# Cutting the last slab's first load at 14 of 16 rows, and storing the first slab of a pair in one DMA

## The chip, the cores and the metric

One core of one Trainium2 chip. The metric is the device time of one execution in microseconds (us); lower is better. All runs told of here were in the fast state, and all results were correct.

## The reference

The input is 96 images (32 x 3) of 256 x 256 float32; each is turned by 90 degrees.

```python
def setup_inputs():
    batch, c, h, w = 32, 3, 256, 256
    return {"x": np.random.randn(batch, c, h, w).astype(np.float32)}

def reference(x):
    return np.rot90(x, k=-1, axes=(-2, -1)).astype(np.float32)
```

There is no arithmetic. 25.17 MB are read, rearranged on the chip and 25.17 MB are written.

## The kernel before

The images are cut into 12 slabs of 2 MiB. All slabs fit on the chip at once, so the DMA queue first takes all loads, then all stores; VectorE transposes a slab while others are in flight, and ScalarE makes one last pair of copies. A slab is moved in one of two forms: "short" is 8 rows a partition on 128 partitions, 8 KB a packet; "long" is 16 rows a partition on 64 partitions, as two DMAs (`i` = 0, 1) of 1 MiB with 16 KB a packet. Slabs 0 to 2 are loaded short and stored long, 3 to 7 the other way round, 8 to 11 long both ways.

```python
    long_st = (0, 1, 2)
    both = (8, 10)                       # slabs 8, 9 and 10, 11 are turned in pairs
    paired = [n + a for n in both for a in range(2)]
    # ... (views, tiles, pools)
    for n in (0, 1, 2, 3, 7, 4, 5, 6, *range(8, n_slabs)):
        # ... slabs 1 and 2: one DMA each
        for i in range(I):
            if n in long_st:
                ld = nc.sync.dma_start(out=fours(units[n])[:, i], in_=ld_short[n][:, i])
            else:
                ld = nc.sync.dma_start(out=units[n][i::I], in_=ld_long[n, i])
            if (n, i) == (last, 0):
                mark = ld
    # ... turn(n): the transposes of a slab or a pair
    def store(n):
        if n in paired:
            first = n if n in both else n - 1
            for i in range(I):
                nc.sync.dma_start(out=st_long[n, i], in_=pairs[both.index(first)][n - first :: I, i])
        # ... other slabs
    # ...
    for n in (4, 3, 5, 6, 7, 1, 2):
        st = store(n)
        if n == 4:
            tc.add_manual_dep(st.ins, mark.ins.name, ...)   # "stores after loads"
    for n in range(both[0], n_slabs):
        turn(n)
        store(n)
    # ... slab 0 last, through ScalarE
```

The mark: the first store on the queue (slab 4's) does not wait for its own data, which VectorE has ready at about 46.7 us, but for the first of the last slab's two loads to land.

## Time and profile before

| | before |
|---|---|
| time, median of 3 runs | 123.25 us (123.25 to 123.33) |
| span of the profiled run | 121.5 us |
| bytes moved | 50.33 MB |
| DMA packets | 4752, of which 656 are completions of 4 bytes (41 DMAs x 16 engines) |
| VectorE | busy 90.6 us, done at 99 us |

From the page of the kernel before:

```profile
DVE 90.6 (75%) x24; ACT 4.9 (4%) x3; POOL 0.2 (0%) x4
...
DMA packets 4752, 50.33 MB, mean 414 GB/s; under 512 B 656, under 2 KB 656, under 8 KB 656
```

50.33 MB at 428 GB/s alone are 117.6 us. The rest is start and end: the first packet runs at 1.8 us, the rate is still 139 GB/s from 2 to 3 us, the last one ends at 120.3 us, its completion is seen at 120.65 us and the span closes 0.85 us later. A DMA's issue is an instruction of the queue's sequencer; its bytes move later, on 16 DMA engines (most loads land 19.6 us after their issue). Two readings must be kept apart from here on: "no engine idle" (at every moment 16 packets are on record) and "no packet stretched" (a 16 KB packet takes its usual 611 or 612 ns).

### The profile page before, as it was taken

The page shows a single profiled execution, that of the slowest core. Times are in us where ns is not written, and L with a number is a line of the kernel's source. Part 1 is how long each engine was busy: PE and PEld are TensorE (multiplying, and loading weights), DVE is VectorE, ACT ScalarE, POOL GpSimd, SP SyncE. Part 2 cuts the span into 40 slices and gives each one's busy share as a digit, 9 for nine tenths or more (in the row PEclk, how much of TensorE's full clock was granted, in tenths as well). Part 3 has the DMA queues.
Part 4 walks back from the last instruction along what each step waited for, and adds up shares of the span by engine and source line. Part 5 has one row for each costly group of instructions (what it writes and reads, how often), then busy time and mean ns, then how long its engine had stood idle before and what let it go on. Part 6 is the DMA issues. An engine that isn't in the chain of part 4 may idle for free.

```text
span 121.5 us, 134 instructions
## 1 busy us (share of the span) xinstructions
DVE 90.6 (75%) x24; ACT 4.9 (4%) x3; POOL 0.2 (0%) x4
## 2 busy tenths in 40 slices
DVE  0029999999999999999999999999999960000000
ACT  0000000000000000000040000000000038000000
POOL 0000000000000000000000000000000000000000
DMA  3999999999999999999999999999999999999994
GB/s 73 426 429 426 432 458 426 426 421 421 432 432 432 421 432 432 426 426 432 432 405 426 421 429 431 432 423 431 453 432 432 432 432 432 432 432 432 432 432 173
DMA packets 4752, 50.33 MB, mean 414 GB/s; under 512 B 656, under 2 KB 656, under 8 KB 656
## 3 DMA queue, kind: packets, MB, share of 16 engines
q1 hardware_dynamic: 4752, 50.33, 97.9%
HBM read 25.17 MB, written 25.17 MB: 414 GB/s over the span
## 4 chain that ended last, share of the span: by engine, by line
DVE 59%; issue 13%; DMA 6%; DVEq 3%; ACT 2%; ACTq 1%; SPq 0%
DVE u L116 53%; DVE turned L116 6%; DMA u<-in_x_dram 6%; DVEq L169 3%; ACT u L141 2%; ACTq L169 1%; SPq L92 0%; DVEq L116 0%
## 5 line engine op out<-in xcount | busy, mean ns | idle before, releaser
L116 DVE STREAM_TRANSPOSE u<-u 128x2048 f32<-128x2048 f32 x22 | 83.5, 3866 | 0.3
L116 DVE STREAM_TRANSPOSE turned<-u 128x2048 f32<-128x2048 f32 x2 | 7.1, 3586 | 8.2 <-DMA u<-in_x_dram 8.2
L141 ACT COPY u<-turned 128x2048 f32<-128x2048 f32 x2 | 3.6, 1869 | 35.6 <-DVE u L116 35.6
L141 ACT ACT_TABLE_LOAD x1 | 1.3, 1283 | 62.2 <-DMA u<-in_x_dram 62.2
L158 POOL MEMSET const-bfloat16-1.0<- 128x1 bf16 x1 | 0.1, 101 | 0.0
L158 POOL MEMSET const-uint8-127<- 128x1 uint8 x1 | 0.1, 101 | 0.0
L158 POOL MEMSET const-float32-0.0<- 128x1 f32 x1 | 0.1, 98 | 0.2 <-issue 0.2
L158 POOL MEMSET const-float32-1.0<- 128x1 f32 x1 | 0.1, 98 | 0.0
## 6 DMA issues: line engine op xcount, KB each, us to landing
u<-in_x_dram SPq DMA_DIRECT2D x20, 1024.0 KB, 19.6
out_dram<-u SPq DMA_DIRECT2D x14, 1024.0 KB, 15.6
out_dram<-u SPq DMA_DIRECT2D x5, 2048.0 KB, 16.0
u<-in_x_dram SPq DMA_DIRECT2D x2, 2048.0 KB, 13.7
```

Of the source, the lines that this page charges most:

```text
L116: nc.vector.transpose(out=dst[:, h * step : (h + 1) * step], in_=src[:, h * step : (h + 1) * step])
L141: nc.scalar.copy(out=fours(units[last])[:, i], in_=fours(turned0)[:, i])
L158: nc = _bacc.Bacc("TRN2", target_bir_lowering=False, num_devices=1)
L169: with _tile.TileContext(nc) as tc:
```

## The change

Its intent: let the first store start a little earlier, so that the engines never run dry between loads and stores, without giving up the order "stores after loads"; and issue fewer, larger stores for the pairs.

```diff
             if n in long_st:
                 ld = nc.sync.dma_start(out=fours(units[n])[:, i], in_=ld_short[n][:, i])
             else:
-                ld = nc.sync.dma_start(out=units[n][i::I], in_=ld_long[n, i])
-            if (n, i) == (last, 0):
-                mark = ld
+                cuts = (0, 14 * W, RL * W) if (n, i) == (last, 0) else (0, RL * W)
+                for f0, f1 in zip(cuts, cuts[1:]):
+                    ld = nc.sync.dma_start(out=units[n][i::I, f0:f1], in_=ld_long[n, i][:, f0:f1])
+                    if f1 == 14 * W:
+                        mark = ld
 ...
         if n in paired:
             first = n if n in both else n - 1
+            if n == first:
+                nc.sync.dma_start(out=st_long[n].transpose([1, 0, 2]), in_=pairs[both.index(n)][::I])
+                return
             for i in range(I):
```

## The prediction

> **What bounds the kernel now.** I read the page from the top: the span is 121.5 us, the timed median 123.25 us, so 1.75 us lie outside the span and nothing in the change touches them. Then the 40 slices, the queue and the issues.
>
> ```profile
> DVE  0029999999999999999999999999999960000000
> DMA  3999999999999999999999999999999999999994
> GB/s 73 426 429 426 432 458 426 426 421 421 432 432 432 421 432 432 426 426 432 432 405 426 421 429 431 432 423 431 453 432 432 432 432 432 432 432 432 432 432 173
> ...
> q1 hardware_dynamic: 4752, 50.33, 97.9%
> ...
> u<-in_x_dram SPq DMA_DIRECT2D x20, 1024.0 KB, 19.6
> out_dram<-u SPq DMA_DIRECT2D x14, 1024.0 KB, 15.6
> out_dram<-u SPq DMA_DIRECT2D x5, 2048.0 KB, 16.0
> u<-in_x_dram SPq DMA_DIRECT2D x2, 2048.0 KB, 13.7
> ```
>
> The reader is to see one full row, DMA, from slice 1 to 38, while VectorE stops at about 99 us and the rest of the span, 22 us, is DMA alone. The DMA engines are taken for 97.9% of the whole span. The chain of waits gives 59% of the span to VectorE, and I do not follow it: it walks back through transposes, but when the last transpose ends the queue still holds stores for 20 us. What has to move is 50.33 MB, and only fewer bytes, a higher rate or less idle time of the 16 engines can shorten it.
>
> So the question is whether the engines ever idle at the places that the change touches. The stage table around the change from loads to stores, at about 61 us (columns: stretch, its length, busy time of VectorE, ScalarE and GpSimd, TensorE clock, DMA share, GB/s):
>
> ```profile
> 20.00:60.00 40.00, 39.83 (x11) 0.00 (x0) 0.00 (x0) 1.00 1.01 428
> 60.00:62.00 2.00, 2.00 (x1) 0.00 (x0) 0.00 (x0) 1.00 0.96 406
> 62.00:102.00 40.00, 37.03 (x11) 4.12 (x3) 0.00 (x0) 1.00 1.01 431
> 61.00:61.50 0.50, 0.50 (x1) 0.00 (x0) 0.00 (x0) 1.00 0.71 295
> 57.00:57.50 0.50, 0.50 (x1) 0.00 (x0) 0.00 (x0) 1.00 1.15 492
> ```
>
> At first sight there is a dent where stores take over: 406 against 428 GB/s over 2 us, worst 295 in half a microsecond. That dent is what the change aims at, worth about 2 x (1 - 406/428) = 0.10 us. But the last row warns of the reading: a share of 1.15 of 16 engines is impossible, so a packet is put down whole in the stretch in which it starts, and the sizes change here (16 KB load packets, about 0.61 us each, to 8 KB store packets, about 0.31 us). I therefore followed the trace's packet records engine by engine. Each engine ends its last load's packet, then its 4-byte completion packet (9 ns on record, about 6 ns to the next start), and its first 8 KB store packet starts 6 ns after that completion packet starts; the earliest engine does this at 61.17 us and the latest at 61.69 us. No engine has a gap there. Nor is there one over 0.03 us anywhere from 18 us to 120.2 us. The dent is binning, not idleness.
>
> How near the store was to being late is the other half. The queue's waits and the timeline:
>
> ```profile
> SPq L94 <- DMA u<-in_x_dram: 30.5, 13, 4.5
> SPq L122 <- DVE u L116: 18.0, 2, 9.6
> SPq L127 <- DMA u<-in_x_dram: 16.7, 1, 16.7
> ```
>
> ```profile
> 0.72 0.88 SPq L92 DMA_DIRECT2D u<-in_x_dram  x2
> ...
> 59.77 10.88 SPq L127 DMA_DIRECT2D out_dram<-u  x5
> 62.24 1.28 ACT L141 ACT_TABLE_LOAD   x1 [62.24 <-DMA u<-in_x_dram]
> ```
>
> The first store is held 16.7 us (the deliberate "stores after loads") and issued at 59.77 us, when the first of the last slab's two loads has landed; the second lands at 62.24 us, 2.47 us later, which is one 1 MiB load at this rate. At the start of the kernel the first load is issued at 0.72 us and the trace's first packet starts at 1.77 us: 1.05 us from issue to data. So store packets could flow from 59.77 + 1.05 = 60.82 us, and the earliest engine runs out of loads at 61.17 us. The margin is already +0.35 us.
>
> **What the Trainium skill says.** "DMA: Bandwidth & Descriptors", section "Where 436 GB/s comes from", puts the ceiling of one core's 16 engines at 435 GB/s; the 428 and 431 GB/s above are 98 to 99% of it, so the trace agrees and there is no rate left to gain. The same page, "Anatomy of one DMA", says the DMA engines never wait on semaphores, only the issuing sequencer does, and that a completion comes after the last byte is confirmed landed: in the trace the mark load's completion packets run at 58.71 to 59.24 us and the wait ends at 59.77 us. Its section on why a DMA increments its semaphore by 16 says the engine count is the largest number up to 16 that divides the slowest dimension: 64 partitions give 16, in the split loads and in the merged store (64 x 2 x 4096, partition outermost); the 656 small packets of the page are 41 DMAs x 16, which agrees. "Perfetto Trace Analysis", section "DMA Optimizations", warns of overhead for DMAs under 2 KB; the new small load moves 2 rows x 1 KB = 2 KB a packet, on that border, and no row of this trace shows that size.
>
> **The change, part by part.** The order of instructions on every engine but the DMA queue's is the same: 24 transposes, 2 copies, unchanged shapes. On the queue there are 40 DMAs for 41.
>
> (1) The mark covers 14 of 16 rows. It lands 2/16 of a load earlier: 2.45 us x 1/8 = 0.31 us, so the first store should be issued at about 59.47 us and the margin becomes 0.66 us. Gain on the path: 0, because the engines had no gap to fill.
>
> (2) The split adds 64 packets, 4 an engine. A 16 KB packet takes 0.612 us, two 8 KB ones 2 x 0.306 us from start to start, so a packet's own overhead is below what I can see, some 5 ns. 4 x 5 ns = 0.02 us, plus one completion packet of 6 ns. All of this is on the path, as every engine's time is: +0.03 us.
>
> (3) Two merged stores remove two completions an engine: -2 x 6 ns = -0.012 us. Packets (16 KB) and bytes stay. They remove two issues, of 0.47 to 1.39 us each, but the issuing queue runs ahead: when the second pair's stores are issued at 99.16 us, 18 MiB have been asked for and (99.16 - 61.4)/2.447 = 15.4 MiB have been moved, so 2.6 MiB or 6.3 us lie in the queue; at the first pair's, 84.73 us, 14 - 9.5 = 4.5 MiB or 11 us. Gain on the path: 0. The stores still wait for all four transposes of their pair, so no transfer starts earlier.
>
> (4) The eight completion semaphores are handed round, so each DMA from the split on waits for another earlier one, eight back. All of those landed long before (loads take 19.6 us to land when eight are queued; the small one shortens the queue by under 1 MiB). Cost 0.
>
> Sum: +0.03 - 0.01 = +0.02 us. 123.25 + 0.02 = 123.27; I round to 123.25, as the three runs before spread over 0.08 us.
>
> **The rivals.** (A) The dent is a real bubble, or one exists in the timed executions that the profiled one does not show: then an earlier first store fills up to 0.10 to 0.15 us and the time is 123.1. For it: the 295 GB/s slice, and that somebody chose 14 rows. Against it: the packet records, the +0.35 us margin and the tight 123.25 to 123.33. (B) The 2 KB packets are dear: if each held an engine as long as an 8 KB one, 4 x (0.31 - 0.08) = 0.9 us, 124.2; at 40 ns extra each 0.16 us, 123.4. Against it: size scaling from 16 to 8 KB is exact. (C) The merged store, with two distant output regions interleaved a partition at a time, could write slower: 5% on two stores of 4.9 us is 0.5 us, 123.7. Against it: the 2 MiB stores of the first stage also have two regions and run at the same 431 GB/s. (D) The longer issue of a merged store starves the queue: it would need over 6.3 us, and issues take at most 1.4 us a MiB.
>
> **Range and chances.** Rival A pulls 0.15 us down, B and C at their mild sizes 0.15 to 0.2 us up, and a run can sit 0.1 us off by itself: 123.0 to 123.45. A gain of over 2% would be 2.4 us, but all idle time of the DMA engines in the whole span is 2.1% of 121.5 = 2.6 us, nearly all in the first 3 and last 1.3 us, which the change does not touch: chance 0.01. A loss of 2.4 us needs B and C at full size and more: 0.01. Within 2%: 0.98.
>
> **What would show it.** In the changed kernel's trace the first store should be issued at 59.4 to 59.5 us, its wait shortened to about 16.4 us, and the last load should still land at 62.2 to 62.3 us. The GB/s dent at 61 us should remain, perhaps moved, because it is the change of packet size; if it is gone and the span is 0.1 us shorter, rival A was right. DMA packets should be 4752 + 64 - 16 = 4800, of which 640 under 512 B, with some 64 more under 8 KB; the queue's share stays at 97.9% give or take 0.2. The last copy's stores and the end of the span should stay at 121.5 us. A span longer by over 0.2 us with a higher share in the slice before 61 us speaks for B, with a lower GB/s from 85 to 110 us for C.

## The result, and the profile after

| | before | after |
|---|---|---|
| time, median of 6 runs | 123.25 us (123.20 to 123.62) | 123.21 us (123.14 to 123.44) |
| ratio | 1 | 0.9994, 95% interval 0.998 to 1.0007 |
| span of the profiled run | 121.5 us | 121.4 us |

All outputs are right. A ratio here is the mean time of one kernel's runs over the mean of the other's in the same rounds, so it is not quite the ratio of the medians. The verdict is "same".

The page after, its lines that answer to those of before:

```profile
DMA  3999999999999999999999999999999999999994
GB/s 84 416 432 424 426 459 432 432 432 426 426 432 426 416 421 432 421 426 450 403 424 426 426 429 429 421 432 424 464 426 432 432 432 432 432 432 432 432 432 178
DMA packets 4800, 50.33 MB, mean 414 GB/s; under 512 B 640, under 2 KB 640, under 8 KB 704
...
q1 hardware_dynamic: 4800, 50.33, 98.0%
...
out_dram<-u SPq DMA_DIRECT2D x7, 2048.0 KB, 16.3
...
u<-in_x_dram SPq DMA_DIRECT2D x1, 896.0 KB, 19.3
u<-in_x_dram SPq DMA_DIRECT2D x1, 128.0 KB, 17.2
```

The two pieces are there (896 KB and 128 KB), so are the two merged stores (seven of 2 MiB, five before), and the packets are the 4800 that were counted ahead. The DMA row and the bandwidth are those of before. The stages around the change from loads to stores (stretch, length, VectorE, ScalarE, GpSimd, clock, DMA share, GB/s):

```profile
20.00:60.00 40.00, 39.83 (x11) 0.00 (x0) 0.00 (x0) 1.00 1.00 426
60.00:62.00 2.00, 2.00 (x1) 0.00 (x0) 0.00 (x0) 1.00 0.94 397
62.00:102.00 40.00, 36.97 (x11) 4.18 (x3) 0.00 (x0) 1.00 1.02 432
61.00:61.50 0.50, 0.50 (x1) 0.00 (x0) 0.00 (x0) 1.00 0.40 164
```

The dent at 61 us is deeper than before (164 against 295 GB/s, 397 against 406 over 2 us) in a kernel that is no slower, and the packet records show 16 packets under way throughout. A dent that grows while nothing idles is a matter of which packet starts in which slice: a DMA share of 0.40 over half a microsecond does not show an idle engine. The queue's waits and the timeline after:

```profile
SPq L96 <- DMA u<-in_x_dram: 32.5, 14, 4.5
...
SPq L132 <- DMA u<-in_x_dram: 13.9, 1, 13.9
```

```profile
59.46 11.13 SPq L132 DMA_DIRECT2D out_dram<-u  x5
62.26 1.28 ACT L146 ACT_TABLE_LOAD   x1 [62.26 <-DMA u<-in_x_dram]
```

The first store is issued at 59.46 us, 0.31 us ahead of before, and the last load lands at 62.26 us against 62.24 us: the lead did not bring the last load in sooner, and the extra pieces cost it 0.02 us.

### The profile page after: what moved, and what is told of

Its sections match the earlier page's. It is cut to its first block, busy times and chain, and to the rows that moved or that the text cites. A ratio compares the mean times of both kernels' runs of the same rounds, so it can differ in the third digit from the quotient of the medians.

```text
span 121.4 us, 134 instructions
## 1 busy us (share of the span) xinstructions
DVE 90.5 (75%) x24; ACT 4.9 (4%) x3; POOL 0.2 (0%) x4
## 4 chain that ended last, share of the span: by engine, by line
DVE 55%; issue 17%; DMA 6%; DVEq 3%; ACT 2%; ACTq 1%; SPq 0%
DVE u L118 50%; DVE turned L118 6%; DMA u<-in_x_dram 6%; DVEq L174 3%; ACT u L146 2%; ACTq L174 1%; SPq L92 0%; DVEq L118 0%
```

## The experiments

Twelve kernels were run. Each differs from the kernel before, unless told otherwise, by the edit shown. "Issued at" is the first slab 4 store's issue, which is what most of them move. Statements on packets and landings come from one profiled execution of each kernel.

### Each half of the change alone

The load split alone (the diff above without its store part):

> The load split alone, stores as before. My theory (the 16 DMA engines have no gap where stores take over from loads): within 0.1 us of the kernel before, worked out as +0.03 us; first store issued at 59.46 us, last load landing at 62.26 us as in the changed kernel. Rival A (the dent in GB/s at 61 us was an idle stretch that the split fills): 0.10 to 0.15 us faster than before, and a dent that is gone.

Measured: 123.39 us (123.29 to 123.48) against 123.29 us, ratio 1.0004 (0.9992 to 1.0016). Issued at 59.40 us.

The merged store alone:

> The merged store alone, loads and mark as before (first store issued at 59.77 us). My theory: within 0.1 us of before, worked out as -0.01 us. Observed after the prediction: in the changed kernel the 16 engines end their last store at slightly more different moments (119.8 to 120.3 us) than before (120.15 to 120.3 us), with a mean about 0.17 us earlier. If the merged store does that, this run shows it and the split alone does not; the end, set by the slowest engine, should still move by under 0.1 us. Rival C (two output regions interleaved write slower): 0.2 to 0.5 us slower.

Measured: 123.26 us against 123.29 us, ratio 0.9995 (0.9982 to 1.0008). Issued at 59.81 us. Neither half moves the time, so the result is not a gain and a loss that cancel. What I had supposed of the merged store found no support: the profiled run of the merged store alone does not end with an earlier mean over the engines (120.61 us, against 120.57 us before and 120.40 us after), while the split alone does (120.38 us). In these profiles the small shift goes with the earlier issue; but the profiled run of the merged store alone was the slowest of its six (123.66 us), so the comparison is a weak one. It is taken up below.

Both slabs of each pair merged, on top of the changed kernel:

```diff
-            if n == first:
-                nc.sync.dma_start(out=st_long[n].transpose([1, 0, 2]), in_=pairs[both.index(n)][::I])
-                return
-            for i in range(I):
-                nc.sync.dma_start(out=st_long[n, i], in_=pairs[both.index(first)][n - first :: I, i])
+            nc.sync.dma_start(out=st_long[n].transpose([1, 0, 2]), in_=pairs[both.index(first)][n - first :: I])
+            return
```

> The changed kernel with both slabs of each pair stored in one 2 MiB store, so four merged stores and 38 DMAs. My theory: bytes and packets are the same, four completions fewer an engine than before the split, so within 0.1 us of the kernel before. If interleaving two output regions cost something (rival C): 0.2 us or more slower. If fewer, larger stores helped: at least 0.1 us faster.

Measured: 123.32 us (123.25 to 123.39) against 123.28 us, ratio 0.9994 (0.9975 to 1.0013). Four merged stores are worth as little as two. Rival C, at 0.2 us or more, is out: the upper ends of the two intervals are +0.10 us (two merged stores) and +0.16 us (four).

### A late first store, so that a real gap can be seen

The first try held only slab 4's store until the very last load:

```diff
-            if (n, i) == (last, 0):
+            if (n, i) == (last, 1):
                 mark = ld
```

> The first store waits for the last load instead of the one before it. My theory of the margin (1.05 us from issue to first data; engines run out of loads between 61.17 and 61.69 us): the first store is issued at about 62.25 us, its data start at about 63.3 us, so a real gap of 1.6 us (slowest engine) to 2.1 us (earliest engine) opens, and the time is 124.8 to 125.4 us. If instead the kernel had slack elsewhere in the DMA stage, or the chain of waits through VectorE set the end, the time would stay within 0.3 us of 123.25.

Measured: 123.44 us, ratio 1.0008 (0.9993 to 1.0023). This did not test what it was meant to: with that mark the schedule put another slab's store, which has no mark, first, and issued it at 45.03 us. It queued behind the loads, so the engines had work when the loads ended. The second try holds every early store (this edit comes on top of the one above):

```diff
-        st = store(n)
-        if n == 4:
+        for st in store(n):          # store() returns the list of its DMAs
             tc.add_manual_dep(st.ins, mark.ins.name, ...
```

> Repeats the late mark, this time with every store held (in the earlier try the schedule issued another unit's store at 45.03 us, so nothing was late). All stores wait for the last load. My theory of the margin: first store issued at about 62.2 us, its data at about 63.25 us (1.05 us later, as at the start of the kernel), while the engines run out of loads at 61.2 to 61.7 us: a gap of about 2.1 us for the earliest engine and 1.6 us for the latest, time 124.8 to 125.4 us. If the chain through VectorE or slack elsewhere set the end: within 0.3 us of 123.25.

Measured: 125.67 us (125.58 to 125.69) against 123.34 us, ratio 1.018 (1.0156 to 1.0204). From its timeline and its stages:

```profile
62.03 8.36 SPq L126 DMA_DIRECT2D out_dram<-u  x5
```

```profile
61.00:63.00 2.00, 1.97 (x2) 0.95 (x1) 0.00 (x0) 1.00 0.08 33
67.00:87.00 20.00, 19.93 (x6) 0.00 (x0) 0.00 (x0) 1.00 1.01 419
```

This is what a true gap looks like: DMA share 0.08 and 33 GB/s for two microseconds. The store was issued at 62.03 us and its first packet runs at 62.94 us, so 0.91 us lie between. The engines ran out at 61.14 to 61.50 us; in engine time 1.63 us were idle. The kernel lost 2.3 us, more than the idle time, and the second line shows where most of the rest went: from 67 to 87 us, with all engines busy, it moves 419 GB/s where the kernel before moves 430. The same two stretches of the kernel before:

```profile
61.00:63.00 2.00, 1.97 (x2) 0.76 (x1) 0.00 (x0) 1.00 0.93 393
67.00:87.00 20.00, 19.93 (x6) 0.00 (x0) 0.00 (x0) 1.00 1.02 430
```

The landings agree: 19.93 us from the first store to the fifth, against 19.50 us before. Half that delay, with every early store held as in the last edit:

```diff
+                cuts = (0, 8 * W, RL * W) if (n, i) == (last, 1) else (0, RL * W)   # mark: the first half
```

> The second load of the last slab cut at 8 rows, every store waits for its first half: the first store is issued 1.22 us later than before, at about 61.0 us, its data at about 62.05 us. My theory of the margin: gaps of about 0.9 us on the earliest engine and 0.35 us on the latest, time 123.6 to 124.2 us. If issue-to-data inside the running queue is shorter than 1.05 us, less.

Measured: 124.54 us (124.50 to 124.87), ratio 1.0096 (1.007 to 1.0121); issued at 60.98 us, first packet at 61.89 us, again 0.91 us. Idle engine time is 0.49 us, the loss 1.2 us. My number was too small again, for the same reason: idle time plus slower stores afterwards (19.89 us from the first store to the fifth).

And a delay that should still have been inside the margin, again with every early store held:

```diff
+                cuts = (0, 2 * W, RL * W) if (n, i) == (last, 1) else (0, RL * W)   # mark: the 2 rows
```

> The other edge of the window: the second load of the last slab cut at 2 rows, every store waits for its small first piece, so the first store is issued about 0.33 us later than in the kernel before, at about 60.1 us. The late runs measured 0.91 us from the first store's issue to its first packet, so data from about 61.0 us, while the engines run out of loads between 61.15 and 61.7 us. My theory of the margin: still no idle engine, time within 0.15 us of before. If the margin of the kernel before were only the few hundredths of a microsecond that rival A needs: idle time at 61 us and 0.2 us or more slower.

Measured: 123.64 us (123.62 to 123.73) against 123.26 us, ratio 1.0032 (1.0018 to 1.0046). Issued at 60.08 us. Half of the expectation held: 16 packets are on record at every moment, so there is no gap. The other half did not: all five executions are 0.36 us or more above the median of before. The loss lies in the store stage. In the traces' completion records (mean over the 16 engines) the first five stores take 19.64 us from the first landing to the fifth, against 19.50 us before, and the last 10 MiB 24.54 us against 24.48 us; the first store lands at 66.82 us in both kernels, the last one at 120.85 us against 120.57 us. The edit also cuts the second load and ties every early store to the mark; neither was run without the delay.

### An early first store

```diff
-            if (n, i) == (last, 0):
+            if (n, i) == (last - 1, 1):
                 mark = ld
```

> The first store waits for the load before the mark, one load of 2.45 us earlier than in the kernel before, eight times as much lead as the split gives. My theory: first store issued at about 57.3 us, time unchanged, within 0.1 us of before. Rival A (a bubble that an earlier first store fills): at least 0.10 us faster. A third possibility, that stores issued among loads disturb the loads: slower by 0.2 us or more.

Measured: 123.54 us (123.48 to 123.64), ratio 1.0018 (1.0003 to 1.0032). Eight times the change's lead gains nothing, which speaks against rival A from the other side; the third possibility came true. Load packets of 16 KB, normally 611 ns, take up to 985 ns from 60.1 us on (0.17 us an engine in sum above 612 ns). Then only the first store early, the rest at the old mark:

> As the earlier mark, but only the first store goes a load early (57.3 us); the others wait for the mark of the kernel before (59.77 us). If the 0.18% of the earlier mark came from the number of stores queued behind unfinished loads (three 2 MiB stores), the stretched load packets at 60 us (up to 985 ns, normal 611) should be gone or a few, time within 0.1 us of before. If one early store is enough, they stay and the time is 0.15 to 0.3 us above before.

Measured: 123.71 us (123.65 to 123.79), ratio 1.0026 (1.0002 to 1.0049). One early store is enough; the number of queued stores is not the cause. The loss is a little above what I gave for this case, and the packets are stretched from 59.0 us on, 0.39 us an engine in sum. The split at 2 rows and at 8 rows of the last slab's first load (the change's edit with 2 or 8 for 14, no merged store) lie between:

> The split at 2 rows, mark on the small first piece: the first store is issued 2.1 us ahead of before, at about 57.6 us, with a load and seven eighths still to come. Between 1.22 us of lead (same time) and 2.45 us (0.18% slower): if the lead itself is what disturbs the last loads, stretched load packets near 60 us and 0.1 to 0.25 us above before; if not, within 0.1 us.

Measured: 123.49 us (123.35 to 123.73), ratio 1.0008 (0.9979 to 1.0036): inconclusive in time. The trace has stretched load packets after 60 us, 0.10 us an engine in sum.

> The split at 8 rows instead of 14, mark on the first half, stores as before: the first store is issued about 1.22 us ahead of the kernel before (58.5 us), between the 0.31 us of the change and the 2.45 us of the earlier mark, which was 0.18% slower and whose trace has load packets of up to 985 ns (normal 611) once stores were queued. If stores queued early stretch the loads' last packets, some such packets show after 60 us and the time is 0.05 to 0.25 us above before; if the slowness of the earlier mark was chance, no packet over 640 ns and the time within 0.1 us.

Measured: 123.27 us (123.23 to 123.36), ratio 0.9988 (0.9967 to 1.0009), and no packet is stretched. Seen in the stages, 57 to 62 us, of the kernel before, the earlier mark, the single early store, the 2-row split and the 8-row split, one line each in that order:

```profile
57.00:62.00 5.00, 5.00 (x2) 0.00 (x0) 0.00 (x0) 1.00 0.99 421
```

```profile
57.00:62.00 5.00, 5.00 (x2) 0.00 (x0) 0.00 (x0) 1.00 0.99 406
```

```profile
57.00:62.00 5.00, 5.00 (x2) 0.00 (x0) 0.00 (x0) 1.00 0.97 377
```

```profile
57.00:62.00 5.00, 5.00 (x2) 0.00 (x0) 0.00 (x0) 1.00 0.94 389
```

```profile
57.00:62.00 5.00, 5.00 (x2) 0.00 (x0) 0.00 (x0) 1.00 1.01 424
```

The share stays between 0.94 and 1 while the rate falls from 421 to 406, 377 and 389 GB/s: engines that are mostly busy with slow packets, where the late store showed engines with none. The rates do not rank the losses: a packet counts whole where it starts, so an edge of the stretch alone can shift such a rate by tens of GB/s (16 packets of 16 KB are 0.26 MB, 52 GB/s over 5 us). The packet records are firmer. They also hold short gaps, which the kernels issued from 58.5 to 60.1 us do not have: 0.08 us an engine in sum for the earlier mark, 0.05 for the single early store and 0.11 for the 2-row split.

The mis-scheduled late mark above is an early store too, queued 14.7 us ahead of the kernel before, though of another slab. It stretched the load packets less (0.03 us an engine in sum, none over 775 ns), and its ratio of 1.0008 is not clear of noise. So the length of the lead alone does not set the stretch.

### What a small packet costs

The last slab's first load in eight pieces of 2 rows, mark on the seventh:

```diff
+                cuts = tuple(range(0, RL * W + 1, 2 * W)) if (n, i) == (last, 0) else (0, RL * W)
```

> The last slab's first load in eight pieces of 2 rows (2 KB packets), mark on the seventh. The changed kernel's trace has 2 KB packets at 84 ns against 611 / 8 = 76.4 ns for the same bytes in a 16 KB packet. My theory of packet overhead: 32 packets an engine x 7.6 ns = 0.24 us plus 7 more completions x 6 ns = 0.04 us, so 0.28 us slower than the kernel before (123.5). If small packets cost nothing on the path: within 0.1 us. If issue or the eight completion semaphores bind instead: a gap before the next load and over 0.5 us slower.

Measured: 124.88 us (124.33 to 125.76), ratio 1.0119 (1.0084 to 1.0154). The size of the small packets was right: the eight pieces land one after the other in 2.71 us where the whole load takes 2.45 us, so 0.27 us more, against my 0.28 us. But the third alternative held as well. Each DMA waits for the one eight places back, and the load after the pieces now waits for the first of them, which has landed on all engines at 57.71 us. From the timeline of this run:

```profile
57.39 1.11 SPq L96 DMA_DIRECT2D u<-in_x_dram  x2
59.76 1.79 SPq L129 DMA_DIRECT2D out_dram<-u  x3
```

The last piece and the last load are issued from 57.39 us on, the load itself at 57.91 us; in the kernel before it was queued at 42.57 us. Its first packets take 1.05 to 1.34 us on most engines instead of 0.61 us, and the worst engine ends its last load 2.4 us after the same load of the kernel before. Idle engine time is only 0.33 us, so most of the loss sits inside packets that are on record. (The profiled execution is the slowest of the six, 125.76 us; part of its loss is one engine that ends 1.1 us after the other fifteen.) The long packets look as if a packet's record can include a wait, which is inferred, not shown. A missing gap is to be believed only where the packets also have their usual length, as they have before and after.

### All of them along one axis

| kernel | first store issued, us | time, us | last 10 MiB of stores, us |
|---|---|---|---|
| one store early | 57.26 | 123.71 | 24.35 |
| earlier mark | 57.28 | 123.54 | 24.35 |
| mark at 2 rows | 57.61 | 123.49 | 24.34 |
| mark at 8 rows | 58.49 | 123.27 | 24.34 |
| split alone | 59.40 | 123.39 | 24.33 |
| changed kernel | 59.46 | 123.21 | 24.33 |
| all pair stores merged | 59.46 | 123.32 | 24.31 |
| before | 59.77 | 123.25 | 24.48 |
| merged store alone | 59.81 | 123.26 | 24.49 |
| slightly late | 60.08 | 123.64 | 24.54 |
| half a load late | 60.98 | 124.54 | 24.55 |
| after the last load | 62.03 | 125.67 | 24.57 |

(The last column is from one profiled run each: mean landing of the last store less that of the store ten 1 MiB earlier. Times of different rows are from different chips in part; compare through the ratios above. The mis-scheduled late mark, 24.34 us, and the eight pieces, 24.39 us, are left out: in the one another slab is stored first, in the other the last load comes late.) The time is flat from 58.5 to 59.8 us and rises on both sides. The kernel before sits on the late end of the flat part, the changed one inside it.

## Why the prediction was right

A forecast of "no change" comes true easily; what tests its mechanism are the runs that moved the first store on purpose.

**The engines had no gap to fill (the reading of the dent, and part 1).** Right, and shown from both sides: an earlier issue by 0.3, 1.3 and 2.5 us did not make the kernel faster beyond noise, and where there was a gap (after the last load), share and rate fell to 0.08 and 33 GB/s over two microseconds. The first store came at 59.46 us for a predicted 59.47.

**The margin of 0.35 us.** Right in kind, mis-sized in its term. I took 1.05 us from issue to data from the first load of the kernel; a store needs 0.91 us in both late runs, which makes the margin 0.49 us on the earliest engine. What the prediction did not have is that no idle engine is not yet no loss: the store issued 0.31 us later leaves no gap and still costs 0.3%.

**The cost of the split (part 2).** Predicted +0.03 us. The 2 KB packets are on record with 84 ns against 611 / 8 = 76 ns, so 8 ns each and not 5; from seven extra pieces the cost is 0.27 / 7 = 0.04 us a piece. In the time of the whole kernel that is too small to be seen. (The skill's passage on DMAs under 2 KB speaks of whole DMAs; the prediction read it for packets. No DMA here is that small.)

**The merged stores (part 3).** Predicted -0.01 us; two and four of them show nothing within intervals of 0.13% and 0.19% either side. Issues were indeed off the path: in the three kernels with merged stores no engine idles from 18 to 119.7 us. One slip in the reading: the last 22 us are not DMA alone, since ScalarE copies until 102.8 us; nothing in the sum rests on it.

**The completion semaphores (part 4).** Cost 0, right for one extra DMA. One forecast of detail missed through it: I expected the wait of the first store at 16.4 us, and the view shows 13.9 us. The last load's issue moved one landing later (45.02 us instead of 42.57 us), so the wait began later. Eight pieces show where this stops being free. (The skill's "Anatomy of one DMA", which the prediction leans on, is written for DMAs issued from GpSimd; this kernel issues from SyncE, and its trace shows the same order, completion packets at 58.71 to 59.24 us and the end of the wait at 59.77 us.)

**Rivals.** A (a real bubble), B (dear small packets) and C (slower interleaved stores) each got a run of their own, and none holds at the size that the prediction gave it for this change. A is the closest call: 0.10 us is about what the times can resolve (the interval of the split alone reaches down to -0.10 us, that of the 8-row split to -0.41 us), and what speaks against it are the packet records of one execution, with no idle engine, and the longer leads that gain nothing more. D (a long issue starves the queue) falls with the traces: a merged store's issue takes 0.60 to 1.41 us, against the 6.3 us that D needs.

**What stays open.** Two small losses have no cause shown; their shapes differ.

First, an early store. Why it stretches the last loads' packets is open, but the traces show how the loss reaches the end: it leaves the engines uneven. In the run with the earlier mark the 16 engines' landings lie 0.31 us apart at the last load but one, 0.57 us at the last load, and 0.75 us at the last store. That last store lands at 120.63 us in the mean over the engines, hardly later than before (120.57 us), but at 120.99 us on the slowest, against 120.65 us. The single early store shows the same (120.65 and 121.06 us). The slowest engine sets the time. The change fits this: its last store lands 0.17 us sooner in the mean, but 0.03 us sooner on the slowest engine.

Second, after a late first store all engines run slower: 19.64 to 19.93 us from the first store to the fifth against 19.50 us before, 24.54 to 24.57 us for the last 10 MiB against 24.48 us. That column separates cleanly at 59.5 to 59.8 us. In the slow traces the 16 engines' landings lie close together at the end (within 0.17 to 0.22 us, except 0.50 us in the merged store alone; 0.36 to 0.76 us in the kernels issued before 59.5 us). That the closeness causes the slowness is only argued.

The medians hide one thing more. Over all rounds, kernels with the old mark (before, and merged store alone) gave 10 of 54 executions at 123.6 us or more, up to 123.93, while the four kernels issued between 58.4 and 59.5 us gave none in 24, with 123.48 as the highest. That count was made after the fact and over several chips; it suggests that the change removes occasional slow executions, and it is not a result of the paired rounds. The closeness does not explain it as far as can be seen: the only one of the ten that has a trace (merged store alone, 123.66 us) ends at 120.61 us in the mean, as before, with one engine 0.30 us behind the other fifteen.

No version that was tried beats both kernels beyond noise. With 117.6 us of bytes at the engines' rate and a start and end that no edit here touches, there is little left for one to gain.

## What to carry to other kernels

Before tuning a hand-over between loads and stores, look at the packets there, not at a rate by slices: a dent in GB/s can be a change of packet size. Over half a microsecond even the DMA share misleads (0.40 here with no engine idle); over two microseconds a true gap was plain (0.08). Where the engines had no gap, an earlier issue gained nothing in time. It bought margin, and only up to a point: in two runs too early cost 0.2 to 0.3%, and too late cost 0.3% before any engine idled. Look at the slowest engine and not at the mean, too, since it sets the end. Cutting a load was cheap here, at 0.04 us a piece, as long as the number of DMAs allowed in flight did not push a later load's issue onto the path.

## What the Trainium skill lacked or had wrong

- "DMA: Bandwidth & Descriptors", section "Latency and other measured facts", gives about 600 ns to the first byte for DMAs of this kind, and does not say from where it counts. Here 0.91 us lie between the start of a store's issue and its first packet (two runs), and 1.05 us for the first load; from the end of the issuing instruction, which takes about 0.4 us, they are 0.5 and 0.6 us. So the figure agrees if it counts from there, and is short by 0.3 to 0.45 us for a margin that counts from the start of the issue.
- "Perfetto Trace Analysis", section "DMA Engine Tracks", says that the slices of a DMA engine show actual busy time without idle time; with a load issued late (eight pieces) 16 KB packets are on record with 1.05 to 1.34 us instead of 0.61 us, so a packet's record may hold a wait (inferred from the length).
- No page has the cost of queueing a store behind unfinished loads on the same queue: 16 KB load packets of up to 985 ns instead of 611 ns, and 0.2 to 0.3% of the time in two runs (0.1%, within noise, in two others).
- No page has the slower pace of stores after a late start: 419 against 430 GB/s from 67 to 87 us (19.93 against 19.50 us from the first store's landing to the fifth's), with all 16 engines busy in both.
